# A trunk layer on one core: the first 512 tokens loaded once and turned on the chip, the beginning in written order

## The chip, the cores and the metric

One core of a Trainium2 chip runs one program. It has five engines that run side by side: PE (TensorE, matmuls), DVE (VectorE), ACT (ScalarE), POOL (GpSimd) and SP (SyncE, which issues the loads here). The metric is the device time of one execution in microseconds (us), lower is better.

## The reference

One layer of a hybrid decoder, on a prompt of 2048 tokens and 8 samples of 8 tokens, 1024 channels, float32.

```python
def _rmsnorm(x, w):
    r = lax.rsqrt(jnp.mean(xf * xf, axis=-1, keepdims=True) + EPS)
    return (xf * r).astype(x.dtype) * w
...
    xn = _rmsnorm(x, p["norm_w"])
    h = jnp.einsum("btd,de->bte", xn, p["w_in"])
    q, k, v, z_a, gate_b, gate_c, h_b, z_b, u, v_c, z_c, g = _split_cols(h)
    q = _rmsnorm(q..., p["q_norm_w"]); k = _rmsnorm(k..., p["k_norm_w"])
...
    a = jnp.einsum("bte,ed->btd", jax.nn.silu(z_a) * y_a, p["w_out_a"])   # y_a: windowed attention
    b = jnp.einsum("bte,ed->btd", jax.nn.silu(z_b) * y_b, p["w_out_b"])   # y_b: gated short convolution
    c = jnp.einsum("bte,ed->btd", jax.nn.silu(z_c) * y_c, p["w_out_c"])   # y_c: spatial gating in chunks
    m = gates[:, :, 0] * a + gates[:, :, 1] * b + gates[:, :, 2] * c
    return x + jnp.einsum("btd,de->bte", m, p["w_o"])
```

## The kernel before

**Numbers.** Each float32 operand of a large matmul is split in two: a rounded high part (a cast on ACT, line 169) and the rest as a low part (a subtraction on DVE, line 170). A product is three matmuls: high x high, high x low, low x high. xh and xl are the two parts of the normalised input, wh and wl those of a weight unit, which arrives as raw.

**Blocks.** The tokens are worked in four super-blocks of 512 (the last has the 64 sample tokens besides). Each goes through keys and values (kv_phase), queries (q_phase), attention and convolution, the spatial gate, the merge gates and the output. Weights come in units of 128 x 1024, three raw buffers deep. PE and SP keep the order in which the program is written. ACT, DVE and POOL are put in order by a scheduler, which may take instructions out of the written order. Small pieces of work are written into the stream of matmuls by a clock of their own: later(delay, piece) queues a piece, and tick runs what is due.

**The beginning.** first_block prepares xh and xl of the first super-block, in four tiles of 128 tokens. Each tile is loaded twice: as xnat, with tokens on the partitions, and as xin, with channels on the partitions (from the transposed copy in_xt). From xnat ACT takes the squares with their sum (line 265), POOL makes of it the factor 1/rms (rstd, lines 165 and 166, the second a power), PE turns the factors round and ACT copies them (xrbuf), and DVE multiplies xin by the norm weight and the factor, 128 columns at a time (line 273), followed by the split into xh and xl. In kv_phase tile i needs xh and xl of its own, and prepare(i + 1) is written into the middle of the matmuls of tile i:

```python
            if prepare and i + 1 < ntile:
                later(0.25, lambda i=i: prepare(i + 1))
            o = natural(ps_mm()[:rows, :256], i, rows, w)
            r = head_rstd(o[:, 0:128], rows, 2, "k")
            ...
            later(1.0, lambda i=i, rows=rows, kd=kd: keys(i, rows, kd))
```

natural is 24 matmuls with the first two weight units. After them comes the tile's key head: squares of the keys on ACT (sq), their sums on DVE (ks), 1/rms on POOL (kr), the scaled keys on DVE (kd, line 365), and the values' two parts (vst, on ACT and then DVE, lines 392 and 393). keys turns the keys on PE and writes kst. The queries (wide, lines 312 to 314) begin with the third weight unit.

Two PSUM buffers (ps_tp) serve all transposes. xin and xnat lie in places that rbuf and sbuf of the attention take later.

Of the kernel before, what the change touches and what calls it, by code (L numbers as in the profile page):

```python
# [10 lines left out]
F32 = mybir.dt.float32  # L11
F32R = mybir.dt.float32r
AF = mybir.ActivationFunctionType
ALU = mybir.AluOpType
AX = mybir.AxisListType

P = 128
D = 1024
# [6 lines left out]
KT = D // P  # L25
SLOPES = [2.0 ** -(h + 1) for h in range(8)]
TMAX = 576
# [21 lines left out]
def trunk_kernel(ctx: ExitStack, tc: tile.TileContext, A, O):  # L49
    nc = tc.nc  # L50
    consts = ctx.enter_context(tc.tile_pool(name="consts", bufs=1))
    res = ctx.enter_context(tc.tile_pool(name="res", bufs=1))
# [9 lines left out]
    def ps_tp():  # L62
        return psum.tile([P, 512], F32, tag="tp", name="ps_tp", bufs=2)

    def tmp(name, shape, tag="tmp", bufs=5):
        n = int(np.prod(shape[1:]))
        assert n <= 580
        t = tmps.tile([P, 580], F32, tag=tag, name=name, bufs=bufs)[:, :n]
        if len(shape) == 3:
            t = t.rearrange("p (a b) -> p a b", a=shape[1])  # L70
        elif len(shape) == 4:
            t = t.rearrange("p (a b c) -> p a b c", a=shape[1], b=shape[2])
        return t
# [9 lines left out]
    def later(delay, fn):  # L83
        heapq.heappush(pending, (clock[0] + delay, len(pieces)))
        pieces.append(fn)
# [6 lines left out]
    def flush():  # L92
        while pending:
            pieces[heapq.heappop(pending)[1]]()
# [20 lines left out]
    def load_to(j):  # L115
        while len(loaded) < min(j, len(units)):
            src = units[len(loaded)][2]
            raw = raws.tile([P, WE], F32, tag="raw", name="raw")
            nc.sync.dma_start(raw[:, : src.shape[1]], src)
            loaded.append(raw)  # L120

    def split_to(j):
        while len(ready) < min(j, len(units)):
            i = len(ready)
            load_to(i + 1)
            n = units[i][2].shape[1]
            wh = wts.tile([P, WE], F32R, tag="wh", name="wh")
            wl = wts.tile([P, WE], F32R, tag="wl", name="wl")
            split(wh[:, :n], wl[:, :n], loaded[i][:, :n])
            loaded[i] = None  # L130
            ready.append((wh, wl))
            load_to(i + 1 + ahead["loads"])
# [11 lines left out]
    def const(name):  # L144
        src = A[name]
        t = consts.tile(list(src.shape), F32, name="c_" + name)
        nc.sync.dma_start(t, src)
        return t
# [5 lines left out]
    xh = res.tile([P, KT, TMAX], F32R, name="xh")  # L154
    xl = res.tile([P, KT, TMAX], F32R, name="xl")
# [7 lines left out]
    def rstd(out, ssq, n, width):  # L163

        nc.gpsimd.tensor_scalar(out, ssq, 1.0 / width, EPS, ALU.mult, ALU.add)
        nc.gpsimd.tensor_tensor(out, out, mhalf[: out.shape[0], :n], ALU.pow)  # L166

    def split(hi, lo, src):
        nc.scalar.copy(hi, src)  # L169
        nc.vector.tensor_tensor(lo, src, hi.bitcast(F32), ALU.subtract)  # L170
# [15 lines left out]
    def t_tiles(j, chunks):  # L186

        w = take("wt", j)
        for c0, c1 in chunks:
            ps = ps_mm()  # L190
            gemm_t(ps, w, KT, *xr, c0, c1)
            yield ps[:, : c1 - c0], c0, c1
# [56 lines left out]
    def first_block():  # L249

        xin = res.tile([P, 8 * TMAX], F32, tag="mh", name="xin")
        xnat = res.tile([P, 8 * TMAX], F32, tag="ml", name="xnat")
        r = small.tile([P, 8], F32, tag="xr", name="xr")
        rbuf = res.tile([P, 4 * TMAX], F32, tag="za", name="xrbuf")
        view = lambda t, i: t[:, i * D:(i + 1) * D].rearrange("p (k t) -> p k t", k=KT)

        def load(i, natural):
            if natural:
                nc.sync.dma_start(xnat[:, i * D:(i + 1) * D], A["xn"][i * P:(i + 1) * P])
            else:  # L260
                nc.sync.dma_start(view(xin, i), A["xt"][:, :, i * P:(i + 1) * P].rearrange("k p t -> p k t"))

        def piece(i):
            sq, x = xnat[:, i * D:(i + 1) * D], view(xin, i)
            nc.scalar.activation(sq, sq, AF.Square, accum_out=r[:, i:i + 1])
            rstd(r[:, i:i + 1], r[:, i:i + 1], 1, D)
            ps = ps_tp()
            nc.tensor.transpose(ps[:, 0:P], r[:, i:i + 1].broadcast_to([P, P]), ident)
            ts = slice(i * P, (i + 1) * P)
            rb = rbuf[:, ts]  # L270
            nc.scalar.copy(rb, ps[:, 0:P])
            for k in range(KT):
                nc.vector.scalar_tensor_tensor(x[:, k], x[:, k], nw[:, k:k + 1], rb, ALU.mult, ALU.mult)
                split(xh[:, k, ts], xl[:, k, ts], x[:, k])
            if i == 3:
                ahead.update(loads=RAWS, splits=AHEAD)

        return load, piece


    def natural(o, i, rows, units, n=256):
# [117 lines left out]
    def q_phase(sb, samp):  # L399
        _, ntile, _, sample = SBS[sb]  # L400
        qn = res.tile([P, 4 * TMAX], F32, tag="br2l", name="qn")
        abuf = samp["abuf"]
        samp["q"] = [x[:NTS, 2048:2304] for x in (qn, abuf)]
        for i, o, rows in wide(2, wide_outs(ntile, sample)):
            r = head_rstd(o, rows, 8, "q")
            for g in range(2):
                gs = slice(g * 256, (g + 1) * 256)
                dst = samp["q"][g] if i == ntile else qn[:, i * 512 + g * 256: i * 512 + (g + 1) * 256]
                nc.vector.scalar_tensor_tensor(  # L409
                    dst.rearrange("p (h d) -> p h d", d=HD),  # L410
                    o[:, gs].rearrange("p (h d) -> p h d", d=HD),
                    HD ** -0.5,
                    r[:rows, 4 * g:4 * g + 4].unsqueeze(2).broadcast_to([rows, 4, HD]),
                    ALU.mult,
                    ALU.mult,
                )
        return qn, abuf
# [338 lines left out]
    def out_phase(sb, m):  # L756
# [11 lines left out]
            nc.sync.dma_start(O["yt"][e, :, t0 * P:t0 * P + n], xt)  # L768
        flush()

    load, prepare = first_block()
    load(0, True)
    nw = const("nw")
    ident = const("ident")
    load_to(1)
    load(0, False)
    load_to(2)
    split_to(1)
    prepare(0)
    split_to(2)  # L780
    for i in range(1, 4):
        load(i, True)
        load(i, False)
    load_to(2 + RAWS)
    knw2 = const("knw2")
    qnw2 = const("qnw2")
# [1 line left out]
    sinkb = const("sinkb")  # L788
# [3 lines left out]
    bsb = const("bsb")  # L792
    sinks_s = const("sinks_s")
    nsinkb = consts.tile([P, 8], F32, name="nsinkb")
    nc.vector.tensor_scalar_mul(nsinkb, sinkb, -1.0)
    nsinks_s = consts.tile([P, 2], F32, name="nsinks_s")
    nc.vector.tensor_scalar_mul(nsinks_s, sinks_s, -1.0)

# [3 lines left out]
    def spatial_weights():  # L804
        wsr = tmp("wsr", [P, 4, P])
        nc.sync.dma_start(wsr, A["wst"])
        nc.gpsimd.affine_select(
            out=wsr, in_=wsr, pattern=[[0, 4], [1, P]], compare_op=ALU.is_ge, fill=0.0, base=0, channel_multiplier=-1
        )
        split(wsp[:, :, 0], wsp[:, :, 1], wsr)  # L810
        nc.scalar.copy(wsp[:, :, 2], wsr)

        nc.gpsimd.memset(wsd, 0.0)
        for n in range(NS):
            nc.sync.dma_start(wsd[n * TS:(n + 1) * TS, :, n * TS:(n + 1) * TS], A["wst"][0:TS, :, 0:TS])
        nc.gpsimd.affine_select(
            out=wsd, in_=wsd, pattern=[[0, 4], [1, NTS]], compare_op=ALU.is_ge, fill=0.0, base=0, channel_multiplier=-1
        )

    for sb in range(len(SBS)):  # L820
        chunks, sample = SBS[sb][2:]
        samp = kv_phase(sb, None if sb else prepare)
        qn, abuf = q_phase(sb, samp)
        flush()
        if not sb:
            spatial_weights()
        za = res.tile([P, 4, TMAX], F32, tag="za", name="za")
        br = [[res.tile([P, 4, TMAX], F32R, tag=f"br{b}{x}", name=f"br{b}{x}") for x in "hl"] for b in range(2)]
        sbuf = attention(sb, qn, abuf, za, br, 0.0, UNIT_EVERY)
        for c in range(4):  # L830
            for ps, c0, c1 in t_tiles(c, chunks):
                nc.scalar.activation(za[:, c, c0:c1], ps, AF.Silu)
        conv_phase(sb, br)
        chunk_phase(sb, br, (samp, sbuf, za, br))
        m = gate_phase(sb, br)
        out_phase(sb, m)
# [124 lines left out]
```

## Time and profile before

| | |
|---|---|
| median of 3 runs | 2047.95 us (2047.21 to 2049.46) |
| the profiled execution | 2048.72 us, its span 2047.0 us |
| PE busy in the span | 2016.7 us (99%) |
| DVE, ACT, POOL busy | 1050.9, 845.8, 83.5 us |
| DMA | 212.25 MB, 104 GB/s in the mean |
| first matmul of the keys | at 11.15 us |
| first matmul of the queries | at 33.27 us, the second at 35.01 |

The span is the time from the first instruction to the last; the execution's own time is a little longer. A row of the order of time gives start, duration, engine, line, operation, tiles (out<-in) and, in brackets, how long the engine was idle before and what ended that. A row of the table of stretches gives from and to, the length, the busy time of PE, PE's weight loads, DVE, ACT and POOL with the count of instructions, the clock that PE was granted, the busy share of the DMA engines and GB/s. A row for one line gives shortest, median and longest duration in ns.

### The profile page before, as it was taken

What the parts mean: (1) busy time and instruction counts of PE and PEld (TensorE: products, weight loads), DVE (VectorE), ACT (ScalarE), POOL (GpSimd) and SP (SyncE); (2) the same over time, 40 slices, a digit from 0 to 9 for tenths busy, and PEclk for the clock granted to TensorE, in tenths of its full rate; (3) what the DMA queues carried; (4) which work ended last, traced back from release to release, by engine and by line L of the source; (5) the groups of instructions that cost most, each with busy time, mean ns of one, the idle gap of its engine ahead of it and who ended that gap; (6) DMA issues with size and microseconds to landing.
All of it is one profiled execution on the core that took longest, in us unless ns stands there. A gap on an engine that the chain in (4) does not pass through costs nothing.

```text
span 2047.0 us, 27359 instructions
## 1 busy us (share of the span) xinstructions
PE 2016.7 (99%) x10887; PEld 1757.1 (86%) x10887; DVE 1050.9 (51%) x1818; ACT 845.8 (41%) x1462; POOL 83.5 (4%) x134
## 2 busy tenths in 40 slices
PE   6999999999999999999999999999999999999999
PEld 5788888888888888888888888888879999999999
DVE  5686263445588353335478535335537842533332
ACT  4675233332476333333267433333247641322320
POOL 2200000000200000000200000000110000000000
PEclk9999999999999999999999999999999998999999
DMA  6222233336222223336322223334522332222233
GB/s 206 82 83 83 84 101 123 114 119 210 84 82 83 88 78 126 111 93 201 119 83 81 84 82 109 118 108 136 173 83 59 64 114 57 65 85 86 78 104 108
DMA packets 85695, 212.25 MB, mean 104 GB/s; under 512 B 18224, under 2 KB 23344, under 8 KB 85552
## 3 DMA queue, kind: packets, MB, share of 16 engines
q1 hardware_dynamic: 85536, 209.53, 33.2%
q8 instruction: 85, 1.39, 0.3%
q10 hardware_dynamic: 32, 0.98, 0.1%
q14 instruction: 42, 0.34, 0.1%
HBM read 201.46 MB, written 10.00 MB: 103 GB/s over the span
## 4 chain that ended last, share of the span: by engine, by line
PE 93%; DVE 3%; ACT 2%; POOL 1%; issue 0%; DMA 0%; SPq 0%; ACTq 0%; DVEq 0%; POOLq 0%
PE ps_mm L179 26%; PE ps_mm L178 26%; PE ps_mm L180 26%; PE ps_tp L488 1%; PE wideS L313 1%; PE wideS L314 1%; PE wideS L312 1%; POOL qr L166 1%; PE ps_mm L312 1%; PE ps_mm L314 1%; PE ps_mm L313 1%; PE sp L464 1%; PE ps_mm L289 1%; PE ps_mm L287 1%; PE ps_mm L288 1%; PE pv L496 1%
## 5 line engine op out<-in xcount | busy, mean ns | idle before, releaser
L178 PE MATMUL ps_mm<-xh,wh 128*128 128x512 f32 (+1 forms) x2080 | 743.3, 357 | 5.0 <-DVE qn L409 4.5
L180 PE MATMUL ps_mm<-xh,wl 128*128 128x512 f32 (+1 forms) x2080 | 734.4, 353 | 0.0
L179 PE MATMUL ps_mm<-xl,wh 128*128 128x512 f32 (+1 forms) x2080 | 734.3, 353 | 0.0
L170 DVE TENSOR_TENSOR wl<-raw,wh 128x1024 fp32r<-128x1024 f32 x376 | 408.0, 1085 | 576.5 <-ACT wh L169 573.8
L169 ACT CAST wh<-raw 128x1024 fp32r<-128x1024 f32 x376 | 353.5, 941 | 772.1 <-PE ps_mm L179 535.4
L178 PEld LDWEIGHTS ps_mm<-xh,wh 128*128 128x128 f32 x2080 | 393.2, 189 | 51.9 <-issue 4.7
L180 PEld LDWEIGHTS ps_mm<-xh,wl 128*128 128x128 f32 x2080 | 392.6, 189 | 49.6
L179 PEld LDWEIGHTS ps_mm<-xl,wh 128*128 128x128 f32 x2080 | 393.4, 189 | 45.7
L179 PE MATMUL ps_mm<-ml,wh 128*128 128x512 f32 (+1 forms) x320 | 112.5, 351 | 0.3 <-DVE ml L170 0.3
L180 PE MATMUL ps_mm<-mh,wl 128*128 128x512 f32 (+1 forms) x320 | 112.4, 351 | 0.0
L178 PE MATMUL ps_mm<-mh,wh 128*128 128x512 f32 (+1 forms) x320 | 112.4, 351 | 0.0
L744 DVE TENSOR_TENSOR t<-ps_mm,t 128x512 f32<-128x512 f32 (+1 forms) x120 | 71.6, 597 | 73.7 <-PE ps_mm L180 73.7
L728 ACT ACTIVATE t<-ps_mm,c_bg 128x512 f32<-128x512 f32 (+1 forms) x120 | 73.0, 609 | 69.5 <-PE ps_mm L180 69.5
L450 ACT ACTIVATE rbuf<-ps_tp,c_qnw 64x256 fp32r<-64x256 f32 x128 | 60.0, 468 | 39.4 <-DVE rbuf L451 33.4
L179 PEld LDWEIGHTS ps_mm<-ml,wh 128*128 128x128 f32 x320 | 60.0, 188 | 8.0 <-DVE ml L170 0.6
L180 PEld LDWEIGHTS ps_mm<-mh,wl 128*128 128x128 f32 x320 | 60.1, 188 | 7.5
L178 PEld LDWEIGHTS ps_mm<-mh,wh 128*128 128x128 f32 x320 | 60.1, 188 | 7.4
L474 ACT ACTIVATE sbuf<-sbuf,nm 128x256 f32<-128x256 f32 (+1 forms) x128 | 62.8, 492 | 7.1 <-DVE nm L471 6.8
L767 DVE TENSOR_TENSOR xt<-ps_mm,xt 128x512 f32<-128x512 f32 (+1 forms) x40 | 23.9, 597 | 75.1 <-PE ps_mm L180 46.2
L179 PE MATMUL ps_mm<-br2l,wh 128*128 128x512 f32 (+1 forms) x160 | 56.5, 353 | 0.4 <-DVE br2l L170 0.2
L180 PE MATMUL ps_mm<-br2h,wl 128*128 128x512 f32 (+1 forms) x160 | 56.3, 352 | 0.0
L179 PE MATMUL ps_mm<-br1l,wh 128*128 128x512 f32 (+1 forms) x160 | 56.2, 352 | 0.0
(212 smaller groups left out, 2703.3 us busy)
## 6 DMA issues: line engine op xcount, KB each, us to landing
raw<-in_wt SPq DMA_DIRECT2D x208, 512.0 KB
raw<-in_wout SPq DMA_DIRECT2D x96, 256.0 KB
raw<-in_wn SPq DMA_DIRECT2D x40, 512.0 KB
raw<-in_wo SPq DMA_DIRECT2D x32, 512.0 KB
xbuf<-in_xn SPq DMA_DIRECT2D x12, 512.0 KB
xt<-in_xt SPq DMA_DIRECT2D x24, 256.0 KB
out_yt<-xt SPq DMA_DIRECT2D x24, 256.0 KB
xbuf<-in_xt SPq DMA_DIRECT2D x16, 256.0 KB
```

The costliest lines, as they stand in the source:

```text
L169: nc.scalar.copy(hi, src)
L170: nc.vector.tensor_tensor(lo, src, hi.bitcast(F32), ALU.subtract)
L178: nc.tensor.matmul(o, wh[:, ws], rh(k, c0, c1), start=k == 0, stop=False)
L179: nc.tensor.matmul(o, wh[:, ws], rl(k, c0, c1), start=False, stop=False)
L180: nc.tensor.matmul(o, wl[:, ws], rh(k, c0, c1), start=False, stop=k == kts - 1)
L312: nc.tensor.matmul(o, xh[:, k, ts], wh[:, ws], start=k == 0, stop=False)
L313: nc.tensor.matmul(o, xh[:, k, ts], wl[:, ws], start=False, stop=False)
L314: nc.tensor.matmul(o, xl[:, k, ts], wh[:, ws], start=False, stop=k == KT - 1)
L450: nc.scalar.activation(hh[half, :, e], src, AF.Copy, scale=qnw2[es])
L474: nc.scalar.activation(s[:, h, k0:], s[:, h, k0:], AF.Exp, bias=nm[:, h:h + 1], accum_out=den[:, h:h + 1])
L728: nc.scalar.activation(t[:, c0:c1], pg[:, : c1 - c0], AF.Sigmoid, bias=bg[:, 8 * b + d:8 * b + d + 1])
L744: nc.vector.tensor_tensor(t[:, c0:c1], pa[:, : c1 - c0], t[:, c0:c1], ALU.mult)
```

## The change

- xin is no longer loaded. Each of the four tiles comes once, as xnat. scale takes the squares (into sqs), the factor as before, and multiplies xnat by it in two halves of 512 channels on DVE. turn transposes the eight 128 x 128 pieces on PE into two PSUM buffers; DVE multiplies each, 512 columns at once, by the norm weight into xin, and splits it.
- The scaling of tile i+1 is written behind the turning of tile i.
- The splits of the third and fourth weight unit are written at 0.5 and 1.0 of the clock behind the last tile.
- nsinkb and nsinks_s are made behind the queries.
- in_order chains all instructions on ACT, DVE and POOL, from the beginning to the end of the query phase of the first super-block, in written order.

```diff
-        def piece(i):
-            sq, x = xnat[:, i * D:(i + 1) * D], view(xin, i)
-            nc.scalar.activation(sq, sq, AF.Square, accum_out=r[:, i:i + 1])
-            rstd(r[:, i:i + 1], r[:, i:i + 1], 1, D)
-            ps = ps_tp()
-            nc.tensor.transpose(ps[:, 0:P], r[:, i:i + 1].broadcast_to([P, P]), ident)
-            ts = slice(i * P, (i + 1) * P)
-            rb = rbuf[:, ts]
-            nc.scalar.copy(rb, ps[:, 0:P])
-            for k in range(KT):
-                nc.vector.scalar_tensor_tensor(x[:, k], x[:, k], nw[:, k:k + 1], rb, ALU.mult, ALU.mult)
-                split(xh[:, k, ts], xl[:, k, ts], x[:, k])
-            if i == 3:
-                ahead.update(loads=RAWS, splits=AHEAD)
+        def load(i):
+            nc.sync.dma_start(xnat[:, i * D:(i + 1) * D], A["xn"][i * P:(i + 1) * P])
+        def scale(i):
+            x = xnat[:, i * D:(i + 1) * D]
+            nc.scalar.activation(sqs[:, i % 2 * D:(i % 2 + 1) * D], x, AF.Square, accum_out=r[:, i:i + 1])
+            rstd(r[:, i:i + 1], r[:, i:i + 1], 1, D)
+            for h in range(2):
+                hs = x[:, h * 512:(h + 1) * 512]
+                nc.vector.tensor_scalar_mul(hs, hs, r[:, i:i + 1])
+        def turn(i):
+            src, x = view(xnat, i), view(xin, i)
+            ts = slice(i * P, (i + 1) * P)
+            pss = []
+            for k0 in (0, 4):
+                ps = ps_tp()[:, :].rearrange("p (k t) -> p k t", k=4)
+                for k in range(4):
+                    nc.tensor.transpose(ps[:, k], src[:, k0 + k], ident)
+                pss.append(ps)
+            for k0, ps in zip((0, 4), pss):
+                ks = slice(k0, k0 + 4)
+                nc.vector.tensor_tensor(x[:, ks], ps, nw[:, ks].unsqueeze(2).broadcast_to([P, 4, P]), ALU.mult)
+                split(xh[:, ks, ts], xl[:, ks, ts], x[:, ks])
+        def piece(i):
+            turn(i)
+            if i + 1 < 4:
+                scale(i + 1)
+            else:
+                later(0.5, lambda: split_to(3))
+                later(1.0, lambda: split_to(4))
+                ahead.update(loads=RAWS, splits=AHEAD)
+    def in_order(begin):
+        last = {}
+        for ins in nc.cur_bb.bb.instructions[begin:]:
+            if ins.engine in last and ins.engine in (
+                mybir.EngineType.Activation, mybir.EngineType.DVE, mybir.EngineType.Pool
+            ):
+                tc.add_manual_dep(
+                    ins,
+                    last[ins.engine],
...
-    load, prepare = first_block()
-    load(0, True)
+    begin = len(nc.cur_bb.bb.instructions)
+    load, scale, prepare = first_block()
+    load(0)
     nw = const("nw")
     ident = const("ident")
     load_to(1)
-    load(0, False)
+    load(1)
     load_to(2)
+    scale(0)
     split_to(1)
+    load(2)
+    load(3)
     prepare(0)
     split_to(2)
-    for i in range(1, 4):
-        load(i, True)
-        load(i, False)
     load_to(2 + RAWS)
...
         if not sb:
+            nc.vector.tensor_scalar_mul(nsinkb, sinkb, -1.0)
+            nc.vector.tensor_scalar_mul(nsinks_s, sinks_s, -1.0)
+            in_order(begin)
             spatial_weights()
```

What this does to the order. ACT at the start, before (xr is the factor, xrbuf the turned factors, an x and a number behind a row count equal ones):

```order
L265 ACTIVATE xnat,xr<-xnat 128x1024
L169 CAST wh<-raw 128x1024
L271 COPY xrbuf<-ps_tp 128x128
L169 CAST xh<-xin 128x128 x2
L169 CAST wh<-raw 128x1024
L169 CAST xh<-xin 128x128 x5
L265 ACTIVATE xnat,xr<-xnat 128x1024
L169 CAST xh<-xin 128x128
```

and after:

```order
L263 ACTIVATE sqs,xr<-xnat 128x1024
L169 CAST wh<-raw 128x1024
L169 CAST xh<-xin 128x4x128 x2
L263 ACTIVATE sqs,xr<-xnat 128x1024
L169 CAST wh<-raw 128x1024
L169 CAST xh<-xin 128x4x128 x2
```

The second tile's square stood ahead of the first tile's last cast; now it stands behind both casts of that tile, and the second weight unit's cast stands behind it.

DVE around the first key head, before:

```order
L273 SCALAR_TENSOR_TENSOR xin<-xin,c_nw,xrbuf 128x128 x4
L170 TENSOR_TENSOR xl<-xin,xh 128x128 x5
L323 TENSOR_REDUCE ks<-sq 128x2
L273 SCALAR_TENSOR_TENSOR xin<-xin,c_nw,xrbuf 128x128 x2
L365 TENSOR_TENSOR kd<-ps_mm,kr 128x256
L273 SCALAR_TENSOR_TENSOR xin<-xin,c_nw,xrbuf 128x128 x3
L393 TENSOR_TENSOR vst<-ps_mm,vst 128x128
L170 TENSOR_TENSOR xl<-xin,xh 128x128 x5
```

and after:

```order
L267 TENSOR_SCALAR xnat<-xnat,xr 128x512 x2
L353 TENSOR_REDUCE ks<-sq 128x2
L395 TENSOR_TENSOR kd<-ps_mm,kr 128x256
L423 TENSOR_TENSOR vst<-ps_mm,vst 128x128
L281 TENSOR_TENSOR xin<-ps_tp,c_nw 128x512
L170 TENSOR_TENSOR xl<-xin,xh 128x4x128
L281 TENSOR_TENSOR xin<-ps_tp,c_nw 128x512
L170 TENSOR_TENSOR xl<-xin,xh 128x4x128
```

Between ks, kd and vst of one tile DVE had other multiplications of the next tile; now the three follow each other, and the next tile's multiplications follow them.

DVE at the third weight unit, before (the row wl is the low part that the queries need first):

```order
L323 TENSOR_REDUCE ks<-sq 128x2
L170 TENSOR_TENSOR xl<-xin,xh 128x128 x2
L365 TENSOR_TENSOR kd<-ps_mm,kr 128x256
L170 TENSOR_TENSOR wl<-raw,wh 128x1024
L393 TENSOR_TENSOR vst<-ps_mm,vst 128x128
```

and after:

```order
L386 SCALAR_TENSOR_TENSOR kst<-ps_tp,c_knw_143,kst 64x2x128
L353 TENSOR_REDUCE ks<-sq 128x2
L395 TENSOR_TENSOR kd<-ps_mm,kr 128x256
L423 TENSOR_TENSOR vst<-ps_mm,vst 128x128
L170 TENSOR_TENSOR wl<-raw,wh 128x1024
```

The unit's subtraction moved from between kd and vst of the third tile to behind them. From the attention of the first super-block on, the rows of all engines are the same in both kernels but for a few around the last queries of the first super-block on DVE.

More of the change, by code (lines that the diff above doesn't have):

```diff
@@ L252, in first_block @@
         xnat = res.tile([P, 8 * TMAX], F32, tag="ml", name="xnat")
+        sqs = res.tile([P, 4 * TMAX], F32, tag="za", name="sqs")
         r = small.tile([P, 8], F32, tag="xr", name="xr")
-        rbuf = res.tile([P, 4 * TMAX], F32, tag="za", name="xrbuf")
         view = lambda t, i: t[:, i * D:(i + 1) * D].rearrange("p (k t) -> p k t", k=KT)
-        def load(i, natural):
-            if natural:
-                nc.sync.dma_start(xnat[:, i * D:(i + 1) * D], A["xn"][i * P:(i + 1) * P])
-            else:
-                nc.sync.dma_start(view(xin, i), A["xt"][:, :, i * P:(i + 1) * P].rearrange("k p t -> p k t"))
@@ L278, in first_block @@
-        return load, piece
+        def load(i):
[7 more added lines that the diff above has]
+                nc.vector.tensor_scalar_mul(hs, hs, r[:, i:i + 1])
@@ new lines, in piece @@
+        def piece(i):
+            turn(i)
+            if i + 1 < 4:
+                scale(i + 1)
+            else:
+                later(0.5, lambda: split_to(3))
+                later(1.0, lambda: split_to(4))
+                ahead.update(loads=RAWS, splits=AHEAD)
+        return load, scale, piece
+    def in_order(begin):
[7 more added lines that the diff above has]
+                    last[ins.engine],
+                    mybir.DependencyInfo(mybir.DependencyClass.NoSync, mybir.DependencyReason.DATA),
+                    reason="in_order",
+                )
+            last[ins.engine] = ins.name
@@ L794, in trunk_kernel @@
     nsinkb = consts.tile([P, 8], F32, name="nsinkb")
-    nc.vector.tensor_scalar_mul(nsinkb, sinkb, -1.0)
     nsinks_s = consts.tile([P, 2], F32, name="nsinks_s")
-    nc.vector.tensor_scalar_mul(nsinks_s, sinks_s, -1.0)
     wsp = consts.tile([P, 4, 3, P], F32R, name="wsp")
```

## The prediction

> **What bounds the kernel now.** I read the page's head and its chain first, then a table of stretches for the beginning, then the order of time there.
>
> ```profile
> span 2047.0 us, 27359 instructions
> PE 2016.7 (99%) x10887; PEld 1757.1 (86%) x10887; DVE 1050.9 (51%) x1818; ACT 845.8 (41%) x1462; POOL 83.5 (4%) x134
> PE 93%; DVE 3%; ACT 2%; POOL 1%; issue 0%; DMA 0%; SPq 0%; ACTq 0%; DVEq 0%; POOLq 0%
> ...
> 0.00:11.10 11.10, 0.47 (x1) 0.18 (x1) 1.89 (x5) 3.94 (x7) 1.29 (x8) 1.00 0.79 263
> 11.10:20.90 9.80, 7.87 (x35) 7.52 (x36) 8.24 (x32) 6.75 (x22) 3.08 (x4) 1.00 1.08 390
> 20.90:35.00 14.10, 10.58 (x71) 8.73 (x70) 11.35 (x44) 10.00 (x31) 4.65 (x11) 1.00 0.24 61
> 35.00:45.00 10.00, 9.99 (x45) 8.15 (x46) 7.82 (x14) 3.00 (x5) 1.72 (x2) 1.00 0.70 195
> ```
>
> TensorE is busy for 99% of the span, and from 35 us on it runs without a gap. So the change can act only through the moment at which this unbroken stream begins. Up to 35 us PE works 0.47 + 7.87 + 10.58 = 18.9 us and idles 16.1 of its 30.3 us (2047.0 - 2016.7). In the third stretch DVE is busy 11.35 of 14.10 us and ACT 10.00: the two together set the pace there. DMA is at 0.24 by then, so loads do not hold it.
>
> **The beginning in order of time**, before (start, duration, engine, line):
>
> ```profile
> 4.23 1.06 ACT L265 ACTIVATE xnat<-xnat 128x1024 f32<-128x1024 f32 x1 [2.15 <-DMA xnat<-in_xn]
> 5.19 0.19 ACT L265 ACTIVATION_READ_ACCUMULATOR xnat<-xnat 128x1 f32 x1
> 5.46 0.19 POOL L165 TENSOR_SCALAR xr<-xr 128x1 f32<-128x1 f32 x1 [4.33 <-ACT xnat L265]
> 5.74 0.56 POOL L166 TENSOR_TENSOR xr<-xr,mhalf 128x1 f32<-128x1 f32 x1
> 8.20 1.04 ACT L169 CAST wh<-raw 128x1024 fp32r<-128x1024 f32 x1 [2.83 <-DMA raw<-in_wn]
> 9.28 1.23 DVE L170 TENSOR_TENSOR wl<-raw,wh 128x1024 fp32r<-128x1024 f32 x1 [8.35 <-ACT wh L169]
> 10.42 0.87 DVE L273 SCALAR_TENSOR_TENSOR xin<-xin,c_nw,xrbuf 128x128 f32<-128x128 f32 x3
> 11.15 0.58 PE L287 MATMUL ps_mm<-wh,xh 128*128 128x256 f32 x1 [4.33 <-ACT xh L169]
> ...
> 33.74 1.22 DVE L170 TENSOR_TENSOR wl<-raw,wh 128x1024 fp32r<-128x1024 f32 x1
> 35.01 0.50 PE L313 MATMUL wideS<-wl,xh 128*128 128x512 f32 x1 [1.26 <-DVE wl L170]
> ```
>
> The stream begins at 35.01, when the low half of the third weight unit (wl, DVE 33.74 to 34.96) is there. The term to be worked out is when that same subtraction ends after the change. Two habits of the rows are used below: on DVE the next instruction starts 0.08 to 0.09 before the reported end of the one ahead (9.28 + 1.23 = 10.51, next at 10.42), and a hand-over to another engine costs 0.04 (ACT 8.20 + 1.04 = 9.24, DVE at 9.28).
>
> **Prices of what is added and removed.**
>
> ```profile
> L621 DVE TENSOR_SCALAR t<-cin,c_cw x16: 477/480/483, 99.8 to 1652.5; 128x512 f32<-128x512 f32 x16
> L744 DVE TENSOR_TENSOR t<-ps_mm,t x120: 448/691/693, 266.1 to 1992.1; 128x512 f32<-128x512 f32 x72, 128x288 f32<-128x288 f32 x48
> 54.90 0.62 ACT L169 CAST wsp<-wsr 128x512 fp32r<-128x512 f32 x1 [0.93 <-POOL wsr L807]
> 55.55 0.69 DVE L170 TENSOR_TENSOR wsp<-wsr,wsp 128x512 fp32r<-128x512 f32 x1 [0.59 <-ACT wsp L169]
> 84.36 0.60 PE L488 MATMUL ps_tp<-c_ident,sbuf 128*128 128x128 f32 x4
> 18.58 1.13 DVE L273 SCALAR_TENSOR_TENSOR xin<-xin,c_nw,xrbuf 128x128 f32<-128x128 f32 x4
> 19.08 1.08 ACT L169 CAST xh<-xin 128x128 fp32r<-128x128 f32 x5
> 19.63 1.09 DVE L170 TENSOR_TENSOR xl<-xin,xh 128x128 fp32r<-128x128 f32 x5
> ```
>
> Per tile of 128 tokens the change removes eight multiplications on DVE (1.13 for four, 2.3), eight casts on ACT (1.08 for five, 1.7), eight subtractions on DVE (1.09 for five, 1.75), one transpose and its copy, and one 512 KB load of xin. It adds two scalings (2 x 0.48, as L621), two multiplications out of PSUM (2 x 0.69, as L744's 128x512), two casts (2 x 0.62), two subtractions (2 x 0.69) and eight transposes (two fours of 0.60). In sum DVE goes from 4.05 to 3.72 us a tile and ACT from 1.96 (with the copy) to 1.24: a little less work. What changes is who waits for whom.
>
> Edits that I cost at nothing: the scalings of tile 0 and its transposes lie between 6.3 and 9.3, while ACT waits for the weight load (8.20) and DVE for wh; without that cover they would cost 0.96 + 0.60. The four loads of xin less make the SP queue shorter and let later units land earlier, but the wait at 35.01 is for DVE, not for a load. nsinkb and nsinks go behind the queries: 0.33 us on a DVE that waits there for POOL. The transposes on PE fall into its idle time at the beginning.
>
> **The new chain.** Before, DVE and ACT have the squares, casts and subtractions of several tiles interleaved; after, both follow the written order, and the square of tile i+1 stands on ACT behind the second cast of tile i, while everything on DVE for tile i+1 stands behind its scaling, which needs that square. One round, from the first multiplication of a tile to that of the next, is then a single file: multiplication 0.69, cast 0.62, subtraction 0.69 (the second multiplication is queued behind it), multiplication 0.69, cast 0.62, square with readout 1.15 (4.23 to 5.38), POOL 0.92 (5.38 to 6.30), two scalings 0.96: 6.34 by durations, 6.15 with the overlaps and hand-overs above. Then:
>
> - Tile 0 starts where it does now, at 10.42, behind wl. Its first matmul comes at 10.42 + 0.69 + 0.62 + hand-overs = 11.8 (11.15 before).
> - Between tiles 0 and 1 stands the second wl: 6.15 + 1.14 = 7.3. Tile 1 at 17.7.
> - Between tiles 1 and 2, and 2 and 3, stands the key head of an earlier tile. Its rows before:
>
> ```profile
> 25.70 0.28 DVE L323 TENSOR_REDUCE ks<-sq 128x2 f32<-128x128 f32 x1
> 26.07 0.19 POOL L165 TENSOR_SCALAR kr<-ks 128x2 f32<-128x2 f32 x1 [2.29 <-DVE ks L323]
> 26.34 0.70 POOL L166 TENSOR_TENSOR kr<-kr,mhalf 128x2 f32<-128x2 f32 x1
> 27.08 0.42 DVE L365 TENSOR_TENSOR kd<-ps_mm,kr 128x256 f32<-128x256 f32 x1 [1.10 <-POOL kr L166]
> 27.54 0.27 ACT L392 CAST vst<-ps_mm 128x128 fp32r<-128x128 f32 x1 [0.64 <-DVE kd L365]
> 28.09 0.28 DVE L393 TENSOR_TENSOR vst<-ps_mm,vst 128x128 fp32r<-128x128 f32 x1
> 33.43 0.98 POOL L424 MEMSET rbuf<- 64x512 f32 x2
> ```
>
> ks to the end of ACT's vst is 25.70 to 27.81, 2.1 us, and DVE's vst adds 0.28. Before, DVE did other tiles' work in POOL's 1.06 us; after, it stands, because kd is next in its queue and the multiplications of the coming tile are behind kd. With the overlap taken off, 2.35: a round of 8.5. Tile 2 at 26.2, tile 3 at 34.8.
> - Behind tile 3: its own two halves, 0.69 + 0.62 + 0.69 + 0.69 + 0.62 + 0.69 = 4.0 by the same rule 4.07, to 38.85. Then key work 0.41, ks to 39.46, POOL (its memsets of rbuf, 0.98, can start only when xin, whose place rbuf takes, is read out at 38.85, and stand ahead of kr: 39.87) 0.98 to 40.9, kd to 41.35, vst on ACT to 41.65, the cast wh of the third unit (1.05) to 42.6 and its wl (1.22) to 43.9.
>
> 43.9 against 34.96 is 8.9 us later. From there PE has the same instructions in the same order as before, and the later rows of ACT and DVE are in the same order too, so the delay is carried to the end.
>
> **The clock at the start of the stream.** PE works in bursts with gaps up to 43.9; from about 40.4 on it has two transposes and one matmul to do. Rows on the granted clock:
>
> ```profile
> 1016.00:1020.00 4.00, 4.00 (x20) 3.27 (x19) 1.79 (x4) 2.37 (x4) 3.21 (x4) 1.00 0.01 4
> 1024.00:1028.00 4.00, 2.65 (x12) 1.81 (x11) 1.62 (x4) 1.99 (x3) 0.75 (x1) 0.98 0.41 127
> 1028.00:1032.00 4.00, 4.00 (x14) 3.29 (x13) 3.92 (x7) 3.06 (x4) 0.00 (x0) 0.59 0.39 110
> 1510.00:1515.00 5.00, 1.70 (x7) 1.73 (x8) 2.31 (x6) 0.00 (x0) 3.66 (x4) 0.75 0.00 0
> ```
>
> After 1.35 us of idle time (1024 to 1028) the clock fell to 0.59 in the next four microseconds: 14 matmuls instead of 20, at 0.2 us each 1.2 us lost. The 1.26 us wait at 35.01 brought no fall. A gap of some 3 us lies nearer to the first and to the 3.3 us at 1510, so I count a loss. Its other bound is the beginning itself, 11.10 to 20.90: PE counts as busy 7.87 us for 35 instructions, 225 ns each, against 149 ns (10.58 for 71) in the next stretch; half as much again. Over the first 20 wide matmuls (0.222 us each, 45 in 9.99) that costs 20 x 0.222 x 0.51 = 2.3. I take the middle of 1.2 and 2.3, 1.7, and keep 0 and twice that as ends.
>
> [...]
>
> **The sum.** 8.9 + 1.7 = 10.6 us. The profiled execution took 2048.72 with its span of 2047.0; it would take 2059.3. It stands 0.77 above the median of the runs, 2047.95, so the median comes to 2058.5, 0.5% slower. Ends of the unknown: the weight load, without xin beside it, may land earlier; issued at 2.17, it cannot come before 5.6 if it takes what the first load took (0.80 to 4.23), and then the scaling and transposes of tile 0 set the start, about 2.1 us sooner. The other way, POOL's steps sometimes last far longer:
>
> ```profile
> 14.45 0.96 POOL L165 TENSOR_SCALAR xr<-xr 128x1 f32<-128x1 f32 x1 [8.15 <-ACT xnat L265]
> 19.58 1.55 POOL L166 TENSOR_TENSOR xr<-xr,mhalf 128x1 f32<-128x1 f32 x1
> ```
>
> 0.96 for 0.19 and 1.55 for 0.56, both beside a busy DVE. After, DVE mostly waits for these very steps, so I take the short values; two or three long ones would add 2 to 3 us.
>
> **Rivals.**
> - Clock kept: the same file, but PE keeps its full clock into the stream. For it the wait at 35.01 without a fall; against it the rows at 1024. 2047.95 + 8.9 = 2056.8. [...] Chance 0.24.
> - Faster: DVE runs without gaps. Its whole work up to the third wl is 8 x 0.48 + 8 x 1.38 + 3 x 1.22 + three key heads of 0.98 + 0.49 = 22.0 us. If the queue never stood still from 9.28 on (the scalings of tile 0 already done), the third wl would end at about 30.3, 4.6 us earlier: 2043.3. It decides for this side if the three rounds come out more than 3.0 us shorter each (8.9 / 3), 5.5 instead of 8.5, for which the next square would have to run under the present tile's casts. The written order on ACT speaks against it. Chance 0.06.
> - Given back later: PE's other 14 us of idle time lie behind 35 us; if half of it were waits for things that the shift does not move, the kernel would end near 2051. Against it: what PE feeds moves with PE. Chance 0.08.
> - Dearer: POOL's long steps in most rounds, 2063 or more. Chance 0.07.
>
> The forecast itself has 0.55. The range 2053 to 2062 takes in the first rival, the earlier weight load and one long POOL step, and leaves out the last three. About 0.2% (4 us) is what a measurement of this kernel can tell from no change: faster 0.05, same 0.09, slower 0.86.
>
> **What the profile after would show.** The first multiplication out of PSUM near 10.4 and those of tiles 1 to 3 near 17.7, 26.2 and 34.8, rounds of 7 to 8.5 us; DVE with waits for POOL's kr and for ACT's casts, and ACT with waits for DVE in each half; the third wl ending near 43.9 and PE without gaps behind it; the clock at half for a few microseconds there. I am wrong if the rounds are near 5 us, or if the squares start before the casts ahead of them end.

## The result and the profile after

The changed kernel takes 2056.77 us in the median (six executions, 2054.86 to 2058.14) against 2048.28 for the kernel before (six, 2047.21 to 2049.54). The ratio is 1.0041, with a 95% interval of 1.0028 to 1.0054: slower, by 0.4%. The execution that was profiled is the fastest of the six, 2054.86 us.

The head of the page of the changed kernel, and its table of stretches for the beginning (columns as before):

```profile
span 2053.1 us, 27344 instructions
PE 2021.2 (98%) x10915; PEld 1761.7 (86%) x10915; DVE 1050.1 (51%) x1778; ACT 842.6 (41%) x1434; POOL 78.8 (4%) x134
...
0.00:11.10 11.10, 2.59 (x10) 2.07 (x10) 3.42 (x7) 4.10 (x5) 1.29 (x8) 1.00 0.80 272
11.10:20.90 9.80, 8.52 (x43) 8.08 (x42) 5.95 (x10) 5.05 (x9) 0.86 (x3) 1.00 0.59 199
20.90:35.00 14.10, 8.93 (x55) 8.21 (x54) 7.17 (x16) 3.60 (x8) 3.15 (x8) 0.82 0.11 37
35.00:45.00 10.00, 7.27 (x38) 6.25 (x38) 5.51 (x11) 3.11 (x9) 2.77 (x6) 0.84 0.16 42
```

DVE and ACT worked 11.35 and 10.00 us of the third stretch before; now they work 7.17 and 3.60. No engine is full, and yet the stretch from 35 to 45, which PE filled before, has 2.7 us of idle time. The order of time shows why (start, duration, engine, line):

```profile
6.87 1.05 ACT L169 CAST wh<-raw 128x1024 fp32r<-128x1024 f32 x1 [1.12 <-DMA raw<-in_wn]
7.95 1.23 DVE L170 TENSOR_TENSOR wl<-raw,wh 128x1024 fp32r<-128x1024 f32 x1 [0.36 <-ACT wh L169]
9.09 0.68 DVE L281 TENSOR_TENSOR xin<-ps_tp,c_nw 128x512 f32<-128x512 f32 x1
10.46 0.69 DVE L170 TENSOR_TENSOR xl<-xin,xh 128x512 fp32r<-128x512 f32 x1 [0.68 <-ACT xh L169]
11.79 0.62 ACT L169 CAST xh<-xin 128x512 fp32r<-128x512 f32 x1 [1.36 <-DVE xin L281]
12.31 1.05 ACT L263 ACTIVATE sqs<-xnat 128x1024 f32<-128x1024 f32 x1
14.40 0.88 DVE L267 TENSOR_SCALAR xnat<-xnat,xr 128x512 f32<-128x512 f32 x2 [1.27 <-ACT wh L169]
16.34 0.69 DVE L281 TENSOR_TENSOR xin<-ps_tp,c_nw 128x512 f32<-128x512 f32 x1
23.83 0.42 DVE L395 TENSOR_TENSOR kd<-ps_mm,kr 128x256 f32<-128x256 f32 x1 [1.10 <-POOL kr L166]
24.79 0.68 DVE L281 TENSOR_TENSOR xin<-ps_tp,c_nw 128x512 f32<-128x512 f32 x1
33.24 0.68 DVE L281 TENSOR_TENSOR xin<-ps_tp,c_nw 128x512 f32<-128x512 f32 x1
37.40 0.98 POOL L454 MEMSET rbuf<- 64x512 f32 x2 [5.17 <-DVE xl L170]
41.19 1.23 DVE L170 TENSOR_TENSOR wl<-raw,wh 128x1024 fp32r<-128x1024 f32 x1 [0.65 <-ACT wh L169]
42.47 0.50 PE L343 MATMUL wideS<-wl,xh 128*128 128x512 f32 x1 [0.76 <-DVE wl L170]
```

In these rows DVE stands in each half of a tile for ACT's cast (0.68), ACT stands for DVE's multiplication (1.36), the square of the next tile starts only behind the second cast (12.31), and DVE stands for its factor (1.27 at 14.40; the row names ACT's wh, which ended at the same time, but what the scaling needs is POOL's xr, 13.81 + 0.55 = 14.36). The stream begins at 42.47, 7.46 us later than at 35.01. The waits of ACT and DVE for each other inside the tiles, added up from 5 to 44 us (waiter, what for, us in all, times, longest):

```profile
ACT xh L169 <- DVE xin L281: 11.9, 8, 2.7
DVE xl L170 <- ACT xh L169: 5.5, 8, 0.7
```

At sixteen hand-overs between ACT and DVE, eight each way, one engine or the other stood still for 17.4 us in all. That is standing time, not time of the kernel: while one of the two stands, the other mostly works.

### The profile page after: what moved, and what is told of

Its sections match the earlier page's. It is cut to its first block, busy times and chain, and to the rows that moved or that the text cites. A ratio compares the mean times of both kernels' runs of the same rounds, so it can differ in the third digit from the quotient of the medians.

```text
span 2053.1 us, 27344 instructions
## 1 busy us (share of the span) xinstructions
PE 2021.2 (98%) x10915; PEld 1761.7 (86%) x10915; DVE 1050.1 (51%) x1778; ACT 842.6 (41%) x1434; POOL 78.8 (4%) x134
## 4 chain that ended last, share of the span: by engine, by line
PE 93%; DVE 3%; POOL 1%; ACT 1%; issue 1%; DMA 0%; SPq 0%; ACTq 0%; DVEq 0%; POOLq 0%
PE ps_mm L178 26%; PE ps_mm L179 26%; PE ps_mm L180 26%; PE ps_tp L518 1%; PE wideS L344 1%; PE wideS L343 1%; PE wideS L342 1%; POOL qr L166 1%; PE ps_mm L342 1%; PE ps_mm L344 1%; PE ps_mm L343 1%; PE sp L494 1%; PE sp L493 1%; PE pv L526 1%; PE pv L525 1%; DVE wl L170 1%
## 5 line engine op out<-in xcount | busy, mean ns | idle before, releaser
L797 DVE TENSOR_TENSOR xt<-ps_mm,xt 128x512 f32<-128x512 f32 (+1 forms) x40 | 23.9, 597 | 75.1 <-PE ps_mm L180 46.9
```

## The experiments

"Tile 0" is the start of the first multiplication of tile 0 into xin, "stream" the start of the first query matmul with the low half (wl), both in the profiled execution; the medians are those of all executions. Ratios are to the kernel before, run beside them, whose median was 2047.50 for the first four kernels and 2047.94 for the last four.

| | tile 0, us | stream, us | median, us | ratio, 95% interval |
|---|---|---|---|---|
| before | 10.42 | 35.01 | 2048.28 | |
| after | 9.09 | 42.47 | 2056.77 | 1.0041 (1.0028 to 1.0054) |
| a1_scheduler_order | 11.79 | 33.52 | 2046.17 | 0.9991 (0.9982 to 0.9999) |
| b1_old_path_in_order | 10.92 | 58.95 | 2074.53 | 1.0130 (1.0115 to 1.0146) |
| c1_both_mults_first | 9.77 | 37.68 | 2050.16 | 1.0014 (1.0005 to 1.0023) |
| d1_squares_ahead | 8.87 | 38.18 | 2053.01 | 1.0023 (1.0015 to 1.0032) |
| e0_both_reorders | 8.99 | 34.06 | 2047.43 | 0.9998 (0.9989 to 1.0006) |
| e1_heads_deferred | 9.88 | 30.28 | 2042.73 | 0.9978 (0.9967 to 0.9988) |
| f1_gap_filled | 9.79 | 43.16 | 2056.18 | 1.0043 (1.0031 to 1.0056) |
| g1_old_loads_kept | 10.47 | 43.87 | 2057.20 (one execution) | |

The median less the stream's start is 2012.4 to 2015.6 in every row. Over 28 us of difference at the beginning, the rest of the kernel took the same time within 3.2 us. That is what the prediction's "the delay is carried to the end" asked for.

**The written order alone, taken away.** The data path of the change stays, and the scheduler orders ACT, DVE and POOL again.

```diff
-            in_order(begin)
```

> The new data path (one load, scaling, transposes) without the chaining in written order: the scheduler orders ACT, DVE and POOL. Theory (the single file of the written order costs the time, the new work does not): squares of later tiles stand ahead of the first casts again, the third unit's wl no longer waits behind three key heads, PE's unbroken stream begins at 31 to 34 us instead of 42.4, and the kernel takes 2044 to 2048 us. Rival (the new work itself, PSUM multiplications and transposes, costs): it stays at 2055 or more with the stream still beginning near 40.

```profile
33.52 0.40 PE L343 MATMUL wideS<-wl,xh 128*128 128x512 f32 x1
```

The stream begins at 33.52, with no wait before it. So everything of the change but the order gains 1.5 us at this point, of which 0.75 may be the first weight unit (its cast started at 7.45, against 8.20 before), and the time gains at most a little (the interval ends at 0.9999). The whole loss, and this gain besides, is the written order: 42.47 - 33.52 = 9.0 us.

**The written order alone, on the old data path.** Two loads a tile, the factors turned and copied, 128 columns at a time; all in written order, with the later parts of the change. The edit is against the kernel before.

```diff
+                later(0.5, lambda: split_to(3))
+                later(1.0, lambda: split_to(4))
...
+            nc.vector.tensor_scalar_mul(nsinkb, sinkb, -1.0)
+            nc.vector.tensor_scalar_mul(nsinks_s, sinks_s, -1.0)
+            in_order(begin)
```

> The old data path (xin loaded, 128 columns at a time) with everything else of the change: written order on ACT, DVE and POOL, the two splits queued, nsinkb behind the queries. Theory: each 128 columns become a single file of 0.35 + 0.30 + 0.28 us with hand-overs, 0.93, eight times a tile 7.4; with square, POOL, transpose, copy (2.9) and the key head (2.3) a round of some 12.7 us; the stream begins near 59 and the kernel takes 2070 to 2076. Rival (the new work is what costs, order is cheap): 2048 to 2052.

```profile
58.95 0.80 PE L331 MATMUL wideS<-wl,xh 128*128 128x512 f32 x1 [0.46 <-DVE wl L170]
```

The order costs this path 58.95 - 35.01 = 23.9 us at the stream and 27 in the median, against 9.0 and 10.6 (2056.77 - 2046.17) for the new path. It has eight multiplication-cast-subtraction files a tile of 0.92 us each (10.92 to 11.84), 7.4 in all, where the change has two of 1.97 (16.34 to 18.31), 3.9. In four tiles that is 14 of the 16.5 us by which its stream is later than that of the change (58.95 - 42.47); tile 0 began 1.8 later too. So what the new path is worth depends on the order: 1.5 us at the stream in the scheduler's, 18 us of time in the written one (2074.53 - 2056.77).

**Single files broken, one at a time.** First, both multiplications of a tile ahead of both splits:

```diff
                 nc.vector.tensor_tensor(x[:, ks], ps, nw[:, ks].unsqueeze(2).broadcast_to([P, 4, P]), ALU.mult)
+            for k0 in (0, 4):
+                ks = slice(k0, k0 + 4)
                 split(xh[:, ks, ts], xl[:, ks, ts], x[:, ks])
```

> The changed kernel with both PSUM multiplications of a tile written ahead of both splits, nothing else. Theory: the second multiplication no longer waits behind the subtraction that waits for the first cast, 1.36 us less a tile, four tiles: the third wl ends near 37.0 instead of 42.4 and the kernel takes 2049 to 2052. Rival (rounds set by POOL and the squares alone): no change, 2056 to 2057.

```profile
9.77 1.28 DVE L281 TENSOR_TENSOR xin<-ps_tp,c_nw 128x512 f32<-128x512 f32 x2
11.14 1.29 DVE L170 TENSOR_TENSOR xl<-xin,xh 128x512 fp32r<-128x512 f32 x2
13.70 0.89 DVE L267 TENSOR_SCALAR xnat<-xnat,xr 128x512 f32<-128x512 f32 x2 [1.27 <-ACT wh L169]
37.68 0.50 PE L345 MATMUL wideS<-wl,xh 128*128 128x512 f32 x1 [0.77 <-DVE wl L170]
```

The first cast now runs under the second multiplication: DVE has no wait inside the tile, and the wait of 1.27 for the factor stands unchanged. The first round is 15.64 - 9.77 = 5.87 instead of 7.25. The stream comes 4.8 us sooner, although tile 0 began 0.7 later here; counted from tile 0 it is 27.9 us instead of 33.4, 5.5 less, for the four times 1.36 that were expected.

Second, square and factor of tile i+1 written ahead of the turning of tile i (the scaling stays behind it):

```diff
...
         def piece(i):
+            if i + 1 < 4:
+                factor(i + 1)
             turn(i)
```

> The changed kernel with the square and 1/rms of tile i+1 written ahead of the turning of tile i, the scaling where it was. Theory: DVE's wait for the factor (1.27 us in three rounds) goes, the rounds become 6.0, 7.2 and 7.2; the third wl ends near 38.7 and the kernel takes 2051 to 2054. Rival (casts are delayed by as much as the square is earlier): no change, 2056 to 2057.

```profile
12.22 0.69 DVE L170 TENSOR_TENSOR xl<-xin,xh 128x512 fp32r<-128x512 f32 x1 [0.69 <-ACT xh L169]
12.83 0.88 DVE L272 TENSOR_SCALAR xnat<-xnat,xr 128x512 f32<-128x512 f32 x2
38.18 0.50 PE L350 MATMUL wideS<-wl,xh 128*128 128x512 f32 x1 [0.75 <-DVE wl L170]
```

Here the reverse: the wait for the cast stands (0.69), that for the factor is gone. The stream comes 4.3 us sooner; counted from tile 0 it is 29.3, 4.1 less. Both edits together:

> The two reorderings of the earlier runs together (both multiplications first, square and factor one tile ahead), still in written order. Theory: the savings add up, since with the multiplications first DVE still waited 1.27 us for the factor in three rounds: the stream begins at 37.7 - 3.8 = 33.9 and the kernel takes 2046 to 2048 us. Rival (they overlap, since ACT then carries square and casts at the same place): the stream stays at 37 or later, 2049 to 2051.

The stream begins at 34.06. Counted from tile 0 it is 25.1, 8.3 less than in the change, of 5.5 + 4.1 = 9.6. Most of the rest is that PE's transposes are now the last to be ready for the second tile: DVE waits for ps_tp 0.92 us ahead of its first multiplication (14.50) and 0.16 ahead of its second. The time is that of the kernel before, so taking out the two single files wins back the whole loss. They are not all that the written order costs: the waits at the key head stand, and the next run takes them out.

**The key head out of the way too.** e0, and in the first super-block kd and vst are written a quarter into the matmuls of the following tile:

```diff
+            if prepare:
+                later(0.26, lambda a=scaled, b=parts: (a(), b()))
+                later(1.0, lambda i=i, rows=rows, kd=kd: keys(i, rows, kd))
+                continue
```

> The same, and in the first super-block kd and vst of a tile are written one tile later, so that DVE works on the next tile while POOL makes kr. Theory: the waits for kr and vst (1.1 + 0.3 us in two rounds, as much behind the last tile) go; the stream begins at 29 to 32 and the kernel takes 2042 to 2046 us, below both kernels. Rival (PE in its slow clock is then the bound of the key stage): the stream stays near 33 to 34, 2046 to 2048.

```profile
23.04 0.42 DVE L406 TENSOR_TENSOR kd<-ps_mm,kr 128x256 f32<-128x256 f32 x1
30.28 0.50 PE L352 MATMUL wideS<-wl,xh 128*128 128x512 f32 x1 [0.63 <-DVE wl L170]
...
35.00:45.00 10.00, 10.00 (x46) 8.04 (x45) 6.19 (x10) 4.08 (x6) 0.00 (x0) 1.00 0.70 212
```

In the two key heads ahead of the third wl, kd (23.04 and 26.77) waits for nothing: POOL's 1.06 us run under DVE's other work, and only the 0.33 for ACT's vst is left. The stream begins at 30.28, and PE is full at full clock in the stretch from 35 to 45. This version beats both kernels: 0.9978 (0.9967 to 0.9988) of the kernel before, about 5 us, and about 14 less than the change as it was made.

**The clock at the start of the stream.** The change, with 12 matmuls that compute nothing wanted, of 512 columns each, in the gap ahead of the first query matmul:

```diff
+            if taken[0] == 3:
+                for f in range(12):
+                    nc.tensor.matmul(outs[0][0], xh[:, f % 4, 0:P], xh[:, f % 4, 0:512], start=True, stop=True)
```

> The changed kernel with 12 matmuls of 512 columns more, ahead of the first query matmul, into the buffer that this matmul then begins anew; they only fill PE's gap between 39.2 and 42.4. Theory on the clock (PE's idle gap ahead of the stream brings the half-clock stretch at 43.5): the stretch goes, the stream still begins at 42.5, about 1.7 us less, 2054.5 to 2056. Rival (the stretch comes from the idle time further ahead, or by chance): the stretch stays, 2056 to 2058.

```profile
39.44 3.00 PE L339 MATMUL wideS<-xh 128*128 128x512 f32 x12
43.16 0.50 PE L346 MATMUL wideS<-wl,xh 128*128 128x512 f32 x1 [0.49 <-DVE wl L170]
...
35.00:45.00 10.00, 9.29 (x54) 7.75 (x53) 5.49 (x10) 3.17 (x8) 2.76 (x6) 0.99 0.06 18
```

The granted clock of that stretch is 0.99 where the change had 0.84: with PE's gap filled the clock did not fall there. This is one execution, and in d1 the clock held over an unfilled gap (last section), so it speaks for idle time of PE as the cause and does not prove it. The time does not show it: the medians are 2056.18 and 2056.77. In this execution the first weight unit came 0.7 us later (its cast at 7.57, against 6.87), as the stream did, and the clock fell at two places where it held in the change: the granted clock is 0.50 from 79.61 to 83.03 and from 557.48 to 560.89, and 1.00 there in the change. So the 1.7 us are shown as a state of the clock, not as time of the whole kernel.

**The old loads beside the new path.** Four loads that nothing reads, of 512 KB each from in_xt, at the places of those removed; the load of tile 1 goes behind that of the second weight unit:

```diff
     load_to(1)
+    idle_load(0)
+    load_to(2)
     load(1)
-    load_to(2)
+    idle_load(1)
...
```

> The changed kernel that still issues the four loads of the transposed copy at their old places, into buffers that nothing reads. Theory (the first weight unit came 1.3 us earlier because the load of xin no longer ran beside it): ACT casts it at 8.2 instead of 6.9, everything behind moves by 1.3, the stream begins near 43.8. Rival (it came earlier for another reason, or by chance): 6.9 and 42.5 stay.

```profile
8.25 1.04 ACT L169 CAST wh<-raw 128x1024 fp32r<-128x1024 f32 x1 [2.79 <-DMA raw<-in_wn]
43.87 0.79 PE L343 MATMUL wideS<-wl,xh 128*128 128x512 f32 x1 [0.58 <-DVE wl L170]
```

The cast starts at 8.25, as in the kernel before (8.20), and the stream is 1.4 us later than in the change, as the theory of the loads had it. But it is one execution, and the others speak against so simple a cause: without those loads the cast started between 6.65 (d1) and 7.66 (e1), and in b1, which has the old loads, at 7.04. What sets the landing of the first weight unit stays open.

## Why the prediction came out right

The kernel became slower by the mechanism that was named, within the range; the time was forecast 1.7 us too high. By its own steps:

- **Tile 0 at 10.42: the step that was off.** It came at 9.09, its first matmul at 10.48 instead of 11.8. The first weight unit was there at 6.87, not at 8.20. The prediction had costed the shorter queue at nothing and named this landing only as its low bound, up to 2.1 us; 1.33 came true. In the executions with a trace it lay between 6.65 and 8.25, so the fixed value was a draw from a spread. The run g1 shows that nothing else was missed at this end: its first cast started at 8.25, tile 0 came at 10.47 for the 10.42 forecast, and the third wl ended at 42.59 + 1.23 = 43.82 for 43.9.
- **The rounds.** 16.34 - 9.09 = 7.25, 24.79 - 16.34 = 8.45, 33.24 - 24.79 = 8.45, for 7.3, 8.5 and 8.5. c1 and d1 took one single file each out of them and, counted from tile 0, moved the stream by 5.5 and 4.1, priced at 5.4 and 3.8.
- **The tail.** From tile 3's first multiplication to the end of wl: 33.24 to 42.42, 9.18 us, for 9.1. POOL's memsets stood ahead of kr as foreseen (37.40 to 38.38, kr at 38.48).
- **The sum.** 7.46 for 8.9; the difference of 1.4 is the landing, nearly alone.
- **Clock.** 1.7 us were counted. The rows in the last section show half clock from 43.55 to 46.96: 3.41 us at 0.50, so 1.7 lost. That the clock would fall was right; that the middle of two bounds, 1.2 and 2.3, met the loss is luck. In the traces it came in whole stretches of 3.41 us at half clock: at the start of the stream one in the change, c1 and e0 (1.7 us each), two in b1 and g1, and none in the kernel before, a1, d1, e1 and f1.
- **The rivals.** The clock-kept rival gave 2056.8, as it happens the median to 0.1. It is not what happened in the trace: there the clock fell, and the file was shorter by about as much. "Dearer" did not come: POOL's steps took 0.19, 0.55 to 0.56 and 0.70 throughout, with DVE standing still beside them. "Given back later" did not come either, by the table of streams. "Faster" was the right price for another order: a DVE without gaps was to end wl at about 30.3, and in e1 it ended at 29.00 + 1.23 = 30.23, with 2042.73 for 2043.3. That it fits so closely is in part chance: DVE still stands still for 2.4 us there between 9.88 and 30.23, and the scalings take 0.44 each and not 0.48.

**The profiled execution.** It should have been 7.46 + 1.7 = 9.2 us longer and was 6.1 (2054.86 - 2048.72). The rest lies in three later stretches in which the clock had fallen in both kernels; the tables of stretches, before:

```profile
1020.00:1040.00 20.00, 18.65 (x81) 14.99 (x80) 11.84 (x25) 12.38 (x23) 3.20 (x3) 0.91 0.27 79
1505.00:1525.00 20.00, 15.47 (x97) 15.22 (x96) 9.07 (x19) 7.46 (x12) 7.33 (x8) 0.83 0.16 54
1695.00:1715.00 20.00, 20.00 (x131) 18.14 (x130) 3.29 (x5) 2.18 (x4) 0.00 (x0) 0.74 0.12 29
```

and after, 9 us later:

```profile
1029.00:1049.00 20.00, 18.66 (x81) 14.95 (x80) 11.78 (x25) 12.64 (x24) 2.91 (x3) 0.91 0.27 80
1514.00:1534.00 20.00, 15.50 (x109) 15.30 (x108) 10.41 (x21) 7.27 (x13) 7.12 (x7) 0.91 0.17 53
1704.00:1724.00 20.00, 20.00 (x140) 18.34 (x139) 2.53 (x4) 2.22 (x5) 0.00 (x0) 0.83 0.15 53
```

(1 - clock) x 20 adds to 10.4 us before and 7.0 after: 3.4 less, and 9.2 - 3.4 = 5.8; 0.3 is left open. The medians, which mean over such draws, differ by 8.5.

## What to carry to other kernels

On engines that each keep one order, ask of every instruction what stands still behind it: a producer and its consumer on two engines, written piece by piece, make a single file in which each engine waits for the other. Write all of one engine's share of a tile ahead of the other's, and the slow producer (here square, factor and the key head's 1/rms) one tile ahead of its use; with both, the written order came out 5 us ahead of the kernel before instead of 8.5 behind it. And where the bound engine runs unbroken from some moment on, the price of everything before is the shift of that moment (here within 3.2 us, over 28 us of shift): read it off one row and add it to the rest.

## What the runs showed of the hardware

**In the trace of the change the clock changed at fixed steps.** The change's beginning, cut every 3.41 us from the first change of the clock in the trace, at 19.65 (PE busy is the first time after the length, the granted clock the first number behind POOL's):

```profile
19.65:23.06 3.41, 2.21 (x20) 2.02 (x19) 1.77 (x4) 1.21 (x3) 0.93 (x3) 1.00 0.64 180
23.06:26.48 3.42, 1.99 (x17) 1.77 (x15) 1.64 (x4) 0.88 (x2) 0.70 (x1) 1.00 0.00 0
26.48:29.89 3.41, 1.66 (x12) 1.25 (x10) 1.66 (x3) 1.83 (x4) 0.57 (x2) 1.00 0.00 0
29.89:33.30 3.41, 2.62 (x13) 2.65 (x14) 1.77 (x6) 0.27 (x1) 1.06 (x3) 0.50 0.02 5
33.30:36.72 3.42, 3.42 (x18) 3.42 (x18) 2.05 (x5) 1.41 (x3) 0.00 (x0) 0.50 0.00 0
36.72:40.13 3.41, 2.52 (x21) 2.28 (x20) 1.76 (x4) 0.56 (x4) 1.88 (x4) 1.00 0.00 0
40.13:43.55 3.42, 1.58 (x6) 1.09 (x7) 2.29 (x4) 1.57 (x4) 0.19 (x1) 1.00 0.11 10
43.55:46.96 3.41, 3.41 (x11) 2.63 (x10) 1.93 (x4) 2.15 (x3) 0.70 (x1) 0.50 0.42 144
```

Every row has one clock, 1.00 or 0.50, so every change of the clock from 19.65 to 46.96 lies on an edge of this grid. In these rows each clock followed from the row ahead: with 1.66 or 1.58 us busy it fell, with 1.99 or more it stayed, so the fall showed at the next edge, when the gap was over. From half clock, 2.62 us did not bring it back and 3.42 did. Ahead of 19.65 the trace holds no record of the clock, and the 1.00 of the tables is no granted clock there: the key matmuls start 0.21 us apart (17.59, 17.80), as they do at half clock (33.49, 33.70), and 0.12 apart behind 19.65 (19.81, 19.93).

PE's busy time is not the whole of it. In the kernel before, 2.06 us of it from 1024.43 to 1027.84 was followed by half clock. Late in the same kernel, PE counts as busy throughout, with matmuls of 32 columns, and the next stretch has 0.50 all the same:

```profile
1696.85:1700.27 3.42, 3.42 (x31) 2.83 (x30) 0.00 (x0) 0.41 (x1) 0.00 (x0) 1.00 0.52 153
```

What counts as work for the clock is therefore not shown here. Nor do the transposes settle it: 0.83 of the 2.21 us from 19.65 on are transposes (22.23 to 23.06), which leaves 1.38 of other work, and the clock stayed at 1.00, where 1.66 and 2.06 us without a transpose were followed by 0.50.

**So a gap ahead of the stream had two prices.** In c1 PE idled 1.37 us before the first query matmul and 0.77 before the second, and the clock fell (0.83 granted from 35 to 45 us); in d1 it idled 2.21 and 0.75, and it did not (1.00). The stretches of the grid around the gap, one of c1 and two of d1, and two matmuls of d1:

```profile
34.74:38.15 3.41, 1.27 (x6) 0.68 (x5) 2.38 (x4) 1.75 (x4) 0.00 (x0) 1.00 0.00 0
...
32.72:36.13 3.41, 1.76 (x13) 1.43 (x12) 1.65 (x5) 0.56 (x3) 1.88 (x4) 1.00 0.00 0
36.13:39.55 3.42, 1.88 (x7) 1.34 (x8) 2.12 (x4) 1.28 (x3) 0.41 (x2) 1.00 0.17 25
...
36.92 0.51 PE L349 MATMUL wideS<-wh,xh 128*128 128x512 f32 x1 [2.21 <-ACT wh L169]
38.75 0.39 PE L349 MATMUL wideS<-wh,xh 128*128 128x512 f32 x1
```

The matmuls behind d1's longer gap take 0.39 us in the trace, those behind c1's shorter one 0.63 (from 38.31). In c1 both waits lie in one stretch, which leaves 1.27 us of work in it; in d1 an edge at 36.13 cuts the long gap, and its two sides keep 1.76 and 1.88. The numbers lie close: in f1 and g1 stretches with 1.75 and 1.74 us of work (from 25.00 and 25.70) were followed by half clock, as 1.76 in d1 was not. Where the gap lies on the grid would explain the two prices; the grid's place was not varied by itself, so this is argued, not shown. It would also account for executions of one kernel that lie several us apart (e1: 2040.31 to 2048.58).
